# A streaming column sum on one core: tapering the last loads, folding half of the accumulator early, and splitting the final copy

## Chip, cores and metric

The kernel runs on one core of a Trainium2 chip. The metric is the device time in microseconds (us) of that core, as the median of several executions. "Span" is the length of the one profiled execution by the profiler's clock; it is some 1.8 us shorter than the time of the same execution.

## The reference

```python
def setup_inputs():
    batch, seq, dim = 32, 1024, 2048
    return {"grad_output": np.random.randn(batch, seq, dim).astype(np.float32)}

def reference(grad_output):
    return np.sum(grad_output, axis=(0, 1)).astype(np.float32)
```

So 32,768 rows of 2048 fp32 values are summed to one row: 268 MB come in and 8 KB go out.

## The kernel before

The rows come in as 128 buffers of 256 rows, two rows per partition (2 MB each, 16 KB contiguous per partition), through a ring of five buffers. Of each buffer VectorE (DVE) adds the first row of every partition to an accumulator `acc` of 128 x 2048. TensorE (PE) sums the second row over the partitions by a matmul with a column of ones, into the first partition of `ps`, in four chunks of 512 columns. At the end PE folds `acc` into `ps` in the same way, one DVE instruction copies `ps` to `res`, and one transfer sends it out.

```python
    for i in range(NBUF):                                   # NBUF = 128
        buf = sbuf.tile([P, Q, D], f32, tag="inbuf")        # Q = 2, bufs=5
        rows = flat[i * P * Q : (i + 1) * P * Q]
        nc.sync.dma_start(out=buf[:], in_=rows.rearrange("(p q) d -> p q d", p=P))
        for t in range(Q):
            if t % 2 == 0:
                nc.vector.tensor_add(acc[:], acc[:], buf[:, t])
            else:
                pe_quantum(buf[:, t])          # 4 matmuls of 512 columns (line 46)

    for k in range(NK):                        # fold: 4 matmuls on acc (line 66)
        nc.tensor.matmul(ps[0:1, k * 512 : (k + 1) * 512], ones[:],
                         acc[:, k * 512 : (k + 1) * 512], start=not started[k], stop=True)

    res = const.tile([1, D], f32)
    nc.vector.tensor_copy(res[0:1], ps[0:1, :D])            # line 75
    nc.sync.dma_start(out=out[None, :], in_=res[0:1])       # line 76
```

Of the kernel before, what the change touches and what calls it, by code (L numbers as in the profile page):

```python
# [1 line left out]

# [4 lines left out]


@with_exitstack  # L10
def kernel(
    ctx: ExitStack,
    tc: tile.TileContext,
    grad_output: bass.AP,
    out: bass.AP,
):
    nc = tc.nc
    P = nc.NUM_PARTITIONS
    f32 = mybir.dt.float32

    flat = grad_output.flatten_outer_dims()
    N, D = flat.shape
    assert D == out.shape[-1]

    Q = 2
    NBUF = N // (P * Q)
    assert N % (P * Q) == 0
    NK = (D + 511) // 512
    assert D % 512 == 0

    sbuf = ctx.enter_context(tc.tile_pool(name="sbuf", bufs=5))
    const = ctx.enter_context(tc.tile_pool(name="const", bufs=1))
    psum = ctx.enter_context(tc.tile_pool(name="psum", bufs=1, space=bass.MemoryType.PSUM))

    acc = const.tile([P, D], f32)
    ones = const.tile([P, 1], f32)
    nc.vector.memset(acc[:], 0.0)  # L37
    nc.any.memset(ones[:], 1.0)  # L38

    ps = psum.tile([P, NK * 512], f32)  # L40

    started = [False] * NK

    def pe_quantum(q_ap):
        for k in range(NK):
            nc.tensor.matmul(  # L46
                ps[0:1, k * 512 : (k + 1) * 512],
                ones[:],
                q_ap[:, k * 512 : (k + 1) * 512],
                start=not started[k],  # L50
                stop=False,
            )
            started[k] = True

    for i in range(NBUF):
        buf = sbuf.tile([P, Q, D], f32, tag="inbuf")
        rows = flat[i * P * Q : (i + 1) * P * Q]
        nc.sync.dma_start(out=buf[:], in_=rows.rearrange("(p q) d -> p q d", p=P))  # L58
        for t in range(Q):
            if t % 2 == 0:  # L60
                nc.vector.tensor_add(acc[:], acc[:], buf[:, t])  # L61
            else:
                pe_quantum(buf[:, t])

    for k in range(NK):
        nc.tensor.matmul(  # L66
            ps[0:1, k * 512 : (k + 1) * 512],
            ones[:],
            acc[:, k * 512 : (k + 1) * 512],
            start=not started[k],  # L70
            stop=True,
        )

    res = const.tile([1, D], f32)
    nc.vector.tensor_copy(res[0:1], ps[0:1, :D])  # L75
    nc.sync.dma_start(out=out[None, :], in_=res[0:1])


# [1 line left out]
_INS = ['grad_output']  # L80
_OUTS = [((2048,), 'float32')]


# [23 lines left out]
```

## Time and profile before

| what | value | where |
|---|---|---|
| time, median of the first 4 runs | 645.27 us (645.11 to 645.57) | timed runs |
| span of the profiled execution | 643.8 us | page |
| the profiled execution's own time | 645.57 us, 0.36 over the median of all 13 runs (645.21) | timed runs |
| bytes in, mean rate over the span | 268 MB, 417 GB/s | page |
| landing of the last load | 632.1 us | chain of waits |
| from there to the end of the span | 11.7 us | chain, timeline |

These are lines of the page of the kernel before: the span, the busy time of each engine, the busy share of the DMA engines and their rate in 40 equal slices of the span, and the shares of the chain that ended last.

```profile
span 643.8 us, 2622 instructions
...
PE 464.6 (72%) x1032; PEld 76.0 (12%) x1032; DVE 297.4 (46%) x130; POOL 0.3 (0%) x5
...
DMA  8999999999999999999999999999999999999991
GB/s 360 432 430 423 432 429 427 428 429 428 427 428 431 425 428 432 427 428 430 428 428 428 432 426 427 434 425 428 432 425 427 429 430 425 430 431 426 427 433 58
...
DMA 84%; PE 15%; DVE 0%; issue 0%; SPq 0%
```

The DMA engines are busy 90% or more (the digit 9) from the second slice to the last but one, at about 428 GB/s. PE looks busy at 72%, but it waits for loads (174.6 us in all, by the page). The 15% of PE in the chain is misleading: in mid-stream the chain passes through PE because PE frees the buffers (123 of the waits of the queue that issues loads end with PE, 153.3 us in all), and four more loads are then outstanding (a load lands 20.8 us after its issue, one every 4.89 us). The interesting slice is the last, where DMA shows 1 and 58 GB/s: the stream is over and something else still runs.

This is the timeline of the kernel before at its end. The columns are start (us), duration (us), engine, line, operation, output<-inputs, shapes and count; in brackets, how long the engine was idle before it and what ended that. "SPq" is the queue that issues transfers.

```profile
622.39 3.59 PE L46 MATMUL ps<-buf,ones 128*1 128x512 f32 x8 [1.30 <-DMA buf<-in_grad_output_dram]
...
627.29 3.59 PE L46 MATMUL ps<-buf,ones 128*1 128x512 f32 x8 [1.31 <-DMA buf<-in_grad_output_dram]
...
632.16 3.59 PE L46 MATMUL ps<-buf,ones 128*1 128x512 f32 x8 [1.27 <-DMA buf<-in_grad_output_dram]
632.21 2.29 DVE L61 TENSOR_TENSOR acc<-acc,buf 128x2048 f32<-128x2048 f32 x1 [2.57 <-DMA buf<-in_grad_output_dram]
...
635.59 3.60 PE L66 MATMUL ps<-acc,ones 128*1 128x512 f32 x8
...
639.22 2.28 DVE L75 COPY res<-ps 1x2048 f32<-1x2048 f32 x1 [4.72 <-PE ps L66]
641.53 0.31 SPq L76 DMA_DIRECT2D out_dram<-res  x1
```

A buffer lands every 4.89 us. PE needs 3.6 us of that and DVE 2.29, so each waits for the next landing. Each fp32 matmul of 512 columns appears as two records ("x8" for four chunks), called passes below; they start 0.43 us apart.

The chain of waits of the same execution shows the tail without overlaps (start, duration, what):

```profile
611.32 20.79 DMA buf<-in_grad_output_dram
632.11 0.04 issue
632.16 3.59 PE ps L46 x8
635.75 3.45 PE ps L66 x8
639.20 0.02 issue
639.22 2.28 DVE res L75
```

After the last landing come 16 PE passes (7.04 us), the copy (2.28 us), and the output with the end of the program (2.26 us). None of this overlaps a load, so all of it is time that a change can win.

### The profile page before, as it was taken

The page shows a single profiled execution, that of the slowest core. Times are in us where ns is not written, and L with a number is a line of the kernel's source. Part 1 is how long each engine was busy: PE and PEld are TensorE (multiplying, and loading weights), DVE is VectorE, ACT ScalarE, POOL GpSimd, SP SyncE. Part 2 cuts the span into 40 slices and gives each one's busy share as a digit, 9 for nine tenths or more (in the row PEclk, how much of TensorE's full clock was granted, in tenths as well). Part 3 has the DMA queues.
Part 4 walks back from the last instruction along what each step waited for, and adds up shares of the span by engine and source line. Part 5 has one row for each costly group of instructions (what it writes and reads, how often), then busy time and mean ns, then how long its engine had stood idle before and what let it go on. Part 6 is the DMA issues. An engine that isn't in the chain of part 4 may idle for free.

```text
span 643.8 us, 2622 instructions
## 1 busy us (share of the span) xinstructions
PE 464.6 (72%) x1032; PEld 76.0 (12%) x1032; DVE 297.4 (46%) x130; POOL 0.3 (0%) x5
## 2 busy tenths in 40 slices
PE   4776776777777677777767777776777677677766
PEld 0111111111111111111111111111111111111111
DVE  3444544544454454445445444544544454445444
POOL 0000000000000000000000000000000000000000
PEclk9999999999999999999999999999999999999999
DMA  8999999999999999999999999999999999999991
GB/s 360 432 430 423 432 429 427 428 429 428 427 428 431 425 428 432 427 428 430 428 428 428 432 426 427 434 425 428 432 425 427 429 430 425 430 431 426 427 433 58
DMA packets 18446, 268.62 MB, mean 417 GB/s; under 512 B 2049, under 2 KB 2049, under 8 KB 2049
## 3 DMA queue, kind: packets, MB, share of 16 engines
q1 hardware_dynamic: 18434, 268.45, 98.1%
q8 instruction: 8, 0.13, 0.1%
q14 instruction: 4, 0.03, 0.0%
HBM read 268.44 MB, written 0.01 MB: 417 GB/s over the span
## 4 chain that ended last, share of the span: by engine, by line
DMA 84%; PE 15%; DVE 0%; issue 0%; SPq 0%
DMA buf<-in_grad_output_dram 84%; PE ps L46 15%; PE ps L66 1%; DVE res L75 0%; SPq L58 0%
## 5 line engine op out<-in xcount | busy, mean ns | idle before, releaser
L46 PE MATMUL ps<-buf,ones 128*1 128x512 f32 x1024 | 461.2, 593 | 174.6 <-DMA buf<-in_grad_output_dram 174.6
L61 DVE TENSOR_TENSOR acc<-acc,buf 128x2048 f32<-128x2048 f32 x128 | 293.4, 2292 | 338.1 <-DMA buf<-in_grad_output_dram 338.1
L46 PEld LDWEIGHTS ps<-buf,ones 128*1 128x1 f32 x1024 | 75.4, 83 | 559.5 <-DMA buf<-in_grad_output_dram 284.5
L75 DVE COPY res<-ps 1x2048 f32<-1x2048 f32 x1 | 2.3, 2279 | 4.7 <-PE ps L66 4.7
L66 PE MATMUL ps<-acc,ones 128*1 128x512 f32 x8 | 3.6, 592 | 0.0
L37 DVE MEMSET acc<- 128x2048 f32 x1 | 1.8, 1765 | 1.2 <-PEq L91 1.2
L66 PEld LDWEIGHTS ps<-acc,ones 128*1 128x1 f32 x8 | 0.7, 84 | 2.8 <-issue 2.8
L91 POOL MEMSET const-bfloat16-1.0<- 128x1 bf16 x1 | 0.1, 101 | 0.0
L91 POOL MEMSET const-uint8-127<- 128x1 uint8 x1 | 0.1, 101 | 0.0
L38 POOL MEMSET ones<- 128x1 f32 x1 | 0.1, 98 | 0.3 <-POOLq L91 0.3
L91 POOL MEMSET const-float32-0.0<- 128x1 f32 x1 | 0.1, 98 | 0.2 <-issue 0.2
L91 POOL MEMSET const-float32-1.0<- 128x1 f32 x1 | 0.1, 98 | 0.0
## 6 DMA issues: line engine op xcount, KB each, us to landing
buf<-in_grad_output_dram SPq DMA_DIRECT2D x128, 2048.0 KB, 20.8
out_dram<-res SPq DMA_DIRECT2D x1, 8.0 KB
```

The source lines that it names most:

```text
L37: nc.vector.memset(acc[:], 0.0)
L38: nc.any.memset(ones[:], 1.0)
L46: nc.tensor.matmul(ps[0:1, k * 512 : (k + 1) * 512], ones[:], q_ap[:, k * 512 : (k + 1) * 512], start=not started[k], stop=False,)
L61: nc.vector.tensor_add(acc[:], acc[:], buf[:, t])
L66: nc.tensor.matmul(ps[0:1, k * 512 : (k + 1) * 512], ones[:], acc[:, k * 512 : (k + 1) * 512], start=not started[k], stop=True,)
L75: nc.vector.tensor_copy(res[0:1], ps[0:1, :D])
L91: nc = _bacc.Bacc("TRN2", target_bir_lowering=False, num_devices=1)
```

## The change

The intent is to shorten that tail without touching the stream. The change does three things:

1. **Taper the loads.** The last 512 rows come as three loads of 128 rows (1 MB), then the last 128 rows in three column pieces of 0.5, 0.25 and 0.25 MB.
2. **Fold early.** After the fourth-last 2 MB buffer PE folds columns 1024 to 2047 of `acc`. From then on, so in the last three 2 MB buffers and the taper, PE takes those columns of every row directly, and DVE takes columns 0 to 1023 alone. So only two chunks are left to fold at the end.
3. **Split the copy.** ScalarE (ACT) copies columns 1024 to 2047 and then 512 to 1023; DVE copies the last 512.

It also replaces the clearing of `acc` by a copy of the first buffer.

```diff
-    NBUF = N // (P * Q)
+    NBULK = (N - 4 * P) // (P * Q)        # 126
+    SWITCH = NBULK - 4
 ... (helpers: dma() loads rows or a column piece; pe() sums chunks of a row directly; fold() sums chunks of acc)
+    for i in range(NBULK):
+        buf = dma(P * Q, Q)
+        if i == 0:
+            nc.vector.tensor_copy(acc[:], buf[:, 0])
+            pe(buf, 1, LO + HI)                       # LO = chunks 0, 1; HI = chunks 2, 3
+        elif i <= SWITCH:
+            nc.vector.tensor_add(acc[:], acc[:], buf[:, 0])
+            pe(buf, 1, LO + HI)
+            if i == SWITCH:
+                fold(HI, stop=False)
+        else:
+            nc.vector.tensor_add(acc[:, 0:H], acc[:, 0:H], buf[:, 0, 0:H])
+            nc.vector.tensor_add(acc[:, 0:H], acc[:, 0:H], buf[:, 1, 0:H])
+            pe(buf, 0, HI)
+            pe(buf, 1, HI)
+    for _ in range(3):
+        bufc = dma(P, 1)
+        nc.vector.tensor_add(acc[:, 0:H], acc[:, 0:H], bufc[:, 0, 0:H])
+        pe(bufc, 0, HI)
+    bhi = dma(P, 1, dlo=H, dhi=D)
+    b1 = dma(P, 1, dlo=512, dhi=H)
+    b0 = dma(P, 1, dlo=0, dhi=512)
+    pe(bhi, 0, HI, stop=True, doff=H)
+    nc.vector.tensor_add(acc[:, 512:H], acc[:, 512:H], b1[:, 0])
+    fold([1], stop=True)
+    nc.vector.tensor_add(acc[:, 0:512], acc[:, 0:512], b0[:, 0])
+    fold([0], stop=True)
-    nc.vector.tensor_copy(res[0:1], ps[0:1, :D])
+    nc.scalar.copy(res[0:1, H:D], ps[0:1, H:D])
+    nc.scalar.copy(res[0:1, 512:H], ps[0:1, 512:H])
+    nc.vector.tensor_copy(res[0:1, 0:512], ps[0:1, 0:512])
```

## The prediction

> **What bounds the kernel.** The load stream. In the page's slices the DMA engines are 90% or more busy almost throughout, at about 428 GB/s, and the chain of waits is 84% DMA. [...] A 2 MB buffer lands each 4.89 us (timeline: 622.39, 627.29, 632.16). Per buffer PE is busy 3.59 us (eight passes, 0.43 us apart), DVE 2.29 us: both have slack. Bytes do not change, so only the ends of the span can. The start cannot: the first load is issued at 0.73 us, and the removed memset ran before the first landing (8.5 us).
>
> **The tail before** (timeline): last landing 632.16; PE on that buffer to 635.6; fold of acc to 639.19; DVE copy of 2048 elements on one partition, 2.28 us, to 641.5; output DMA and end 2.25 us, 643.8. That is 11.6 us, all critical.
>
> **What the change does.** Last loads shrink (three of 1 MB, 0.5 MB, two of 0.25 MB), columns 1024 to 2047 are folded earlier, and the final copy is split: 1024+512 on ACT, 512 on DVE. Estimates from the durations above, landings spaced by bytes:
> - Smaller loads have smaller packets. [...] no view of this trace shows 2 KB packets. I estimate 0.3 us: last landing 632.4, the last 1 MB load about 629.9. The last load's buffer is free (about 628) 4 us before it must land.
> - PE, not the last load, then bounds the tail. From 629.9: 4 passes for the 1 MB load, 4 for the 0.5 MB load (landed 631.2), 2+2 for the two folds: 12 × 0.43 + 0.16 = 5.3 us, to 635.3. The chain through the last load would be ready earlier: add of 512 elements about 0.65 us, to 633.1, while PE is still on earlier work. Some 1.3 us of the ideal gain is lost to PE's backlog.
> - DVE copy of 512: about 0.65 us (a quarter of 2.28 plus start-up), to 636.0. ACT's copies, about 1.0 and 0.6 us, lie beside PE's last passes.
> - Output DMA and end unchanged, 2.25 us: 638.2.
>
> The early fold (4 passes, 1.7 us) fits in the slack of 1.3 us per buffer; with four loads outstanding it does not starve the stream.
>
> So the span falls by 5.5 us, from 643.8 to 638.2, and the time from 645.27 to about **639.7 us** (0.9% less). Range for 8 in 10: 638.7 to 641.3. Chances: faster by over 2% 0.01, within 2% 0.98, slower 0.01.
>
> **What would show each step.** (1) Landings still 4.89 us apart, the last at 632.2 to 633. (2) PE without idle time from the last 1 MB load's landing to the last fold; that fold waits on PE order, not on DVE. (3) DVE copy near 0.65 us, starting about 635.3. (4) Span ends 2.2 to 2.3 us after the output is issued. (5) The chain's last pieces: a load, PE's passes, a short DVE copy, output.
>
> **What would make it wrong.** Small loads landing over 1.2 us late: then the tail is load, add, fold, copy. PE passes slower than 0.43 us. A late-issued small load that leaves the queue empty. ACT's copies outlasting PE's folds. A table load for ACT that disturbs the start. A gain over 2% (13 us) is not possible: the whole tail is 11.6 us.

## The result, and the profile after

The changed kernel takes 639.79 us (median of 8 runs, 639.57 to 639.99), against 645.21 us (13 runs) for the kernel before. The ratio is 0.9915, with a 95% interval of 0.9906 to 0.9925. Ratios here are not quite the ratio of the medians. The change wins 5.4 us, or 0.85%.

The page of the changed kernel, the same lines as before:

```profile
span 638.0 us, 2640 instructions
...
PE 467.0 (73%) x1032; PEld 76.6 (12%) x1032; DVE 293.9 (46%) x135; ACT 2.8 (0%) x3; POOL 0.3 (0%) x5
...
DMA  8999999999999999999999999999999999999995
GB/s 363 428 430 430 427 428 429 427 426 427 427 428 428 425 430 430 427 429 428 429 428 428 427 426 427 428 428 427 430 428 427 428 428 426 429 430 427 428 422 213
```

The stream's rate is the same, and the busy times hardly differ. What changed is the last slice: the DMA engines are busy for half of it, not for a tenth.

The end of its chain of waits, and then its timeline from the last 1 MB load on (weight loads left out):

```profile
616.14 13.33 DMA buf<-in_grad_output_dram
629.47 0.04 issue
629.52 3.59 PE ps L64 x8
633.11 1.73 PE ps L75 x4
634.84 0.02 issue
634.87 0.68 DVE res L116
```

```profile
629.52 3.59 PE L64 MATMUL ps<-buf,ones 128*1 128x512 f32 x8 [0.44 <-DMA buf<-in_grad_output_dram]
629.57 1.22 DVE L102 TENSOR_TENSOR acc<-acc,buf 128x1024 f32<-128x1024 f32 x1 [1.26 <-DMA buf<-in_grad_output_dram]
...
631.44 0.69 DVE L109 TENSOR_TENSOR acc<-acc,buf 128x512 f32<-128x512 f32 x1 [0.65 <-DMA buf<-in_grad_output_dram]
...
632.05 0.68 DVE L111 TENSOR_TENSOR acc<-acc,buf 128x512 f32<-128x512 f32 x1
...
632.95 1.88 PE L75 MATMUL ps<-acc,ones 128*1 128x512 f32 x4
...
633.15 1.00 ACT L114 COPY res<-ps 1x1024 f32<-1x1024 f32 x1 [631.13 <-PE ps L64]
...
634.06 0.57 ACT L115 COPY res<-ps 1x512 f32<-1x512 f32 x1
634.87 0.68 DVE L116 COPY res<-ps 1x512 f32<-1x512 f32 x1 [2.14 <-PE ps L75]
635.62 0.32 SPq L117 DMA_DIRECT2D out_dram<-res  x1
```

The load in the chain is no longer the last one; it is the last 1 MB load, landed at 629.47. From 629.52 PE runs twelve passes without a gap, to 634.84. The very last load landed at 631.99 (the trace's semaphore events, which `prof` does not list); DVE begins to add it at 632.05, and that add is done at 632.73. PE comes to that chunk's fold only 1.1 us later. So the last load is not what the end waits for: PE's queue of passes is.

The two chains account for the difference (each number is taken or subtracted from lines above):

| part of the tail | before | after | difference |
|---|---|---|---|
| start of PE's last unbroken run | 632.16 | 629.52 | -2.64 |
| PE passes in it | 16: 7.04 us | 12: 5.32 us | -1.72 |
| start of the DVE copy to issue of the output | 2.31 us | 0.75 us | -1.56 |
| issue of the output to end of span | 2.26 us | 2.41 us | +0.16 |
| sum | | | -5.76 (spans, unrounded: -5.75) |

The profiled execution of before was 0.36 us above its median, and this lies in the first row: its loads landed late by about that much (copy_only below has the same loads, in an execution at its median, and its last one landed 0.47 us earlier). Without it the sum is -5.4 us, as the medians say. The start does not enter: PE begins on the first buffer at 8.55 us before and at 8.53 after. ACT's one table load, which the trace puts at the line of its first copy, took 1.28 us from 0.73 on and was over before DVE began on the first buffer at 8.42.

### The profile page after: what moved, and what is told of

Same layout as the page of the kernel before. It is cut to its first block, busy times and chain, and to the rows that moved or that the text cites. A ratio compares the mean times of both kernels' runs of the same rounds, so it can differ in the third digit from the quotient of the medians.

```text
span 638.0 us, 2640 instructions
## 1 busy us (share of the span) xinstructions
PE 467.0 (73%) x1032; PEld 76.6 (12%) x1032; DVE 293.9 (46%) x135; ACT 2.8 (0%) x3; POOL 0.3 (0%) x5
## 4 chain that ended last, share of the span: by engine, by line
DMA 82%; PE 18%; issue 0%; DVE 0%
DMA buf<-in_grad_output_dram 82%; PE ps L64 17%; PE ps L75 1%; DVE res L116 0%
## 5 line engine op out<-in xcount | busy, mean ns | idle before, releaser
L90 DVE TENSOR_TENSOR acc<-acc,buf 128x2048 f32<-128x2048 f32 x122 | 279.6, 2292 | 320.4 <-DMA buf<-in_grad_output_dram 320.4
L95 DVE TENSOR_TENSOR acc<-acc,buf 128x1024 f32<-128x1024 f32 x3 | 3.7, 1225 | 7.4 <-DMA buf<-in_grad_output_dram 7.4
L102 DVE TENSOR_TENSOR acc<-acc,buf 128x1024 f32<-128x1024 f32 x3 | 3.7, 1225 | 2.5 <-DMA buf<-in_grad_output_dram 2.5
L114 ACT COPY res<-ps 1x1024 f32<-1x1024 f32 x1 | 1.0, 1001 | 631.1 <-PE ps L64 631.1
L96 DVE TENSOR_TENSOR acc<-acc,buf 128x1024 f32<-128x1024 f32 x3 | 3.7, 1225 | 0.1
L109 DVE TENSOR_TENSOR acc<-acc,buf 128x512 f32<-128x512 f32 x1 | 0.7, 691 | 0.6 <-DMA buf<-in_grad_output_dram 0.6
L111 DVE TENSOR_TENSOR acc<-acc,buf 128x512 f32<-128x512 f32 x1 | 0.7, 682 | 0.0
```

Of the source, the lines that this page charges most:

```text
L90: nc.vector.tensor_add(acc[:], acc[:], buf[:, 0])
L95: nc.vector.tensor_add(acc[:, 0:H], acc[:, 0:H], buf[:, 0, 0:H])
L96: nc.vector.tensor_add(acc[:, 0:H], acc[:, 0:H], buf[:, 1, 0:H])
L102: nc.vector.tensor_add(acc[:, 0:H], acc[:, 0:H], bufc[:, 0, 0:H])
L109: nc.vector.tensor_add(acc[:, 512:H], acc[:, 512:H], b1[:, 0])
L111: nc.vector.tensor_add(acc[:, 0:512], acc[:, 0:512], b0[:, 0])
```

## Experiments

Theory A says that the tail is the sum in this table and that, in the changed kernel, PE's backlog of passes bounds it. Rival B says that the chain through the last load (land, add, fold, copy) bounds it; then PE work could be added for free and DVE work could not. A second rival asked whether one part alone (the loads, say) brings all the gain. All twelve runs gave right results.

The runs came each with runs of the kernel before on the same chip. The intervals of the ratios are wide, 0.6 to 1.1 us to each side, and overlap from row to row. Differences of 0.6 to 1 us between versions of the changed kernel rest on single runs that do not overlap (639.55 to 639.99 for the changed kernel, 640.38 to 640.79 for pe_plus, 638.82 to 639.29 for presum) and on the traces:

| run | median, us | minus before | ratio to before (95%) |
|---|---|---|---|
| copy_only | 643.63 | -1.52 | 0.9977 (0.9964 to 0.9989) |
| fold_only | 643.35 | -1.80 | 0.9972 (0.9959 to 0.9984) |
| loads_only | 643.05 | -2.10 | 0.9967 (0.9954 to 0.9979) |
| pe_plus | 640.55 | -4.60 | 0.9929 (0.9916 to 0.9943) |
| dve_plus1 | 639.72 | -5.42 | 0.9915 (0.9900 to 0.9930) |
| dve_plus3 | 639.77 | -5.37 | 0.9916 (0.9901 to 0.9931) |
| presum | 639.12 | -6.02 | 0.9906 (0.9892 to 0.9921) |
| presum_out | 639.06 | -6.08 | 0.9905 (0.9888 to 0.9921) |
| dve_chain3 | 640.82 | -4.41 | 0.9932 (0.9919 to 0.9944) |
| after_again (the changed kernel) | 639.78 | -5.45 | 0.9914 (0.9900 to 0.9928) |
| presum_again | 639.17 | -6.06 | 0.9905 (0.9892 to 0.9919) |
| presum_out_again | 638.96 | -6.27 | 0.9903 (0.9889 to 0.9916) |

### One part at a time

**copy_only**: the kernel before with the copy split.

```diff
-    nc.vector.tensor_copy(res[0:1], ps[0:1, :D])
+    nc.scalar.copy(res[0:1, 0:1024], ps[0:1, 0:1024])
+    nc.scalar.copy(res[0:1, 1024:1536], ps[0:1, 1024:1536])
+    nc.vector.tensor_copy(res[0:1, 1536:2048], ps[0:1, 1536:2048])
```

> The kernel before with the final copy alone split (ACT copies 1024 and 512 columns, DVE the last 512). If the three parts of the tail simply add, the last fold still ends 7.0 us after the last landing (639.2 on the profile), then a copy of 0.68 us takes the place of 2.28 us: 1.6 us less, about 643.6 us, span 642.2. If ACT's copies (1.00 and 0.57 us as the changed kernel's profile has them) do not fit beside PE's last passes, the output waits for ACT and the gain is smaller. If all the gain comes from the loads, no change: 645.2 us.

Measured: 1.52 us less. In its timeline the last DVE copy takes 0.68 us, and ACT's second copy ends at 638.5, before that copy starts (638.75).

**fold_only**: the early fold with all loads at 2 MB and one copy.

```diff
 (against the changed kernel)
-    NBULK = (N - 4 * P) // (P * Q)
+    NBULK = N // (P * Q)
 ... (the taper is left out; the last buffer's pe() closes chunks 2 and 3)
+    fold([1, 0], stop=True)
+    nc.vector.tensor_copy(res[0:1], ps[0:1, :D])
```

> The early fold alone: in the last four buffers DVE takes columns 0 to 1023 and PE columns 1024 to 2047, the accumulator's upper half is folded before them, all loads stay 2 MB and one DVE copy of 2048 columns ends it. If PE's passes in order bound the tail, the last landing stays at 632.1 and 12 passes (5.3 us) follow it in place of 16 (7.0 us): 1.7 us less, about 643.5 us. If the early fold held the stream back, the last landing would be later than 632.2 and the gain would be lost.

Measured: 1.80 us less. (The edit changes the last three buffers, not four as the expectation says.) The profile has the last landing at 631.5, and then twelve passes in 5.32 us. The stream was not held back.

**loads_only**: the tapered loads, with the fold of all four chunks at the end and one copy.

```diff
 (against the changed kernel)
-            if i == SWITCH:
-                fold(HI, stop=False)
 ... (SWITCH = NBULK: no drain stage)
-    pe(bhi, 0, HI, stop=True, doff=H)
+    pe(bhi, 0, HI, doff=H)
+    fold(HI, stop=True)
 ...
+    nc.vector.tensor_copy(res[0:1], ps[0:1, :D])      (in place of the three copies)
```

> The smaller last loads alone: three of 1 MB, one of 0.5 MB, two of 0.25 MB, with DVE on columns 0 to 1023 and PE on the rest of them, but no early fold and one DVE copy of 2048 columns. If PE's passes in order bound the tail, PE starts its unbroken run of passes at the landing of the last 1 MB load (629.5) and needs 16 of them: 636.6, then copy 2.28 us: 2.6 us less than before, about 642.6 us. If the chain through the last load counted, the fold of the last columns would wait for DVE's add of the last load (632.7) and end 1.0 us after it, and the gain would be over 5 us (640 us or less).

Measured: 2.10 us less, 0.5 us short of the figure, yet the steps are those expected, as the end of its chain of waits shows:

```profile
629.20 3.59 PE ps L62 x8
632.80 3.45 PE ps L73 x8
636.24 0.02 issue
636.27 2.28 DVE res L111
```

PE starts at the last 1 MB landing and runs 16 passes in 7.04 us. The expectation of 2.6 us was set against the profiled execution of before, which was 0.36 us slower than its median. Its output also took 0.16 us longer from issue to end (2.41 against 2.26). 2.64 - 0.36 - 0.16 is 2.1.

The three parts alone win 1.52 + 1.80 + 2.10 = 5.42 us; the whole change wins 5.42. They add, as parts do that shorten different links of one serial chain; that they agree to the last digit is luck, since each median is good to some 0.1 us. No single part holds the gain.

### Which engine bounds the new tail

**pe_plus**: one matmul more (two passes) before the last folds, into a spare bank.

```diff
     pe(bhi, 0, HI, stop=True, doff=H)
+    nc.tensor.matmul(spare[0:1, :], ones[:], bhi[:, 0, 0:512], start=True, stop=True)
```

> The changed kernel with one more matmul of 512 columns (two passes, 0.86 us) into a spare bank just before the last folds. If PE's backlog bounds the tail, all of it shows: 0.86 us more than the changed kernel, about 640.65 us. If the chain through the last load (land, add, fold, copy) bounds it, as the rival has it, the extra passes fit in front of DVE's last add and the time stays at 639.8 us.

Measured: 4.60 us less than before, where the changed kernel wins 5.42 to 5.45. So the two passes cost about 0.8 us of their 0.86: PE has next to no slack in the tail. B fails here. Lines of its chain of waits, with the added passes in line:

```profile
629.21 3.59 PE ps L65 x8
632.80 0.86 PE spare L110 x2
633.66 1.73 PE ps L76 x4
```

**dve_plus1** and **dve_plus3**: one or three adds more on DVE, into a spare tile.

```diff
     fold([1], stop=True)
+    for _ in range(1):      (3 in dve_plus3)
+        nc.vector.tensor_add(spare[:], b1[:, 0], b1[:, 0])
     nc.vector.tensor_add(acc[:, 0:512], acc[:, 0:512], b0[:, 0])
```

> The changed kernel with one more DVE add of 512 columns (0.6 to 0.7 us, into a spare tile) before DVE's add of the last load. In the changed kernel's profile that last add ends at 632.7, and PE comes to the last fold at 633.8: 1.1 us of slack. If PE's backlog bounds the tail, nothing changes: 639.8 us. If the chain through the last load bounds it, 0.6 to 0.7 us more: 640.4 us.

> The same with three more adds, 1.9 us. If PE's backlog bounds the tail with 1.1 us of slack for DVE, only the part beyond the slack shows: 0.8 us more, about 640.6 us, and the last fold's first pass then waits for DVE. If the chain through the last load bounds it, all 1.9 us: 641.7 us.

Measured: dve_plus1 costs nothing (-5.42), as A has it, though DVE's add of the last load started 0.6 us later than in the changed kernel (632.65 against 632.05):

```profile
632.05 0.68 DVE L113 TENSOR_TENSOR spare<-buf 128x512 f32<-128x512 f32 x1
632.65 0.68 DVE L114 TENSOR_TENSOR acc<-acc,buf 128x512 f32<-128x512 f32 x1
```

dve_plus3 costs nothing either (-5.37), and A had expected 0.8 us. Its timeline of DVE shows why:

```profile
631.55 0.69 DVE L110 TENSOR_TENSOR acc<-acc,buf 128x512 f32<-128x512 f32 x1 [0.65 <-DMA buf<-in_grad_output_dram]
632.16 0.69 DVE L113 TENSOR_TENSOR spare<-buf 128x512 f32<-128x512 f32 x1
632.76 0.69 DVE L114 TENSOR_TENSOR acc<-acc,buf 128x512 f32<-128x512 f32 x1
633.37 1.41 DVE L113 TENSOR_TENSOR spare<-buf 128x512 f32<-128x512 f32 x2
```

The add of the last load (line 114) stands second: in the program as built, two of the three spare adds come behind it, and nothing in the source forbade that order. The run was thus no test of three adds. An experiment that adds work must tie it into the chain by data.

**dve_chain3**: the same, mended. The three extra instructions now write what the last add reads.

```diff
     fold([1], stop=True)
+    nc.vector.tensor_sub(zero[:], b1[:, 0], b1[:, 0])
+    nc.vector.tensor_add(acc[:, 0:512], acc[:, 0:512], zero[:])
+    nc.vector.tensor_add(acc[:, 0:512], acc[:, 0:512], zero[:])
     nc.vector.tensor_add(acc[:, 0:512], acc[:, 0:512], b0[:, 0])
```

> The run with three extra DVE adds, mended: there the compiler put two of them behind the add of the last load, so it delayed nothing. Here the three (b1 minus b1, and its zeros added to the accumulator twice) write and read what the last add needs, and so must stand before it. The last add then ends at about 634.7 in place of 632.7, and PE is ready for the last fold at 633.8. If PE's backlog bounds the tail with 1.1 us of slack for DVE, only the part beyond the slack shows: the fold's two passes (1.02 us) follow at 635.8 in place of 634.85, 0.8 to 1.0 us more than the changed kernel of the same call. If the chain through the last load bounds it, all 2.0 us.

> The changed kernel itself, as control of this call: 639.8 us, ratio to before 0.9915.

Measured: 1.04 us more than the changed kernel beside it (640.82 against 639.78). DVE's last add started 1.94 us later than in that control (634.01 against 632.07), and the span of that execution was 0.92 us longer than the control's (638.96 against 638.04), so about 1.0 us of the delay was slack, near the 1.1 us read off the changed kernel's timeline. Lines of its timeline:

```profile
634.01 0.69 DVE L115 TENSOR_TENSOR acc<-acc,buf 128x512 f32<-128x512 f32 x1
...
634.75 1.02 PE L76 MATMUL ps<-acc,ones 128*1 128x512 f32 x2 [1.01 <-DVE acc L115]
635.81 0.68 DVE L120 COPY res<-ps 1x512 f32<-1x512 f32 x1 [1.11 <-PE ps L76]
```

Now PE does wait, 1.01 us, for DVE. This is what B's world looks like, and it had to be made. It also shows the two kinds of bracket: in the changed kernel the passes of the folds carry no wait at all, here there is one of a microsecond.

### A version with less PE work in the tail

If PE's passes bound the tail, taking two away should help. In **presum** the 0.5 MB piece comes as two of 0.25 MB. For chunk 2 DVE, which has slack, adds the last 1 MB load's row to the last block's row first, and PE sums the two rows in one matmul.

```diff
-    for _ in range(3):
+    for n in range(3):
         bufc = dma(P, 1)
         nc.vector.tensor_add(acc[:, 0:H], acc[:, 0:H], bufc[:, 0, 0:H])
-        pe(bufc, 0, HI)
+        pe(bufc, 0, HI if n < 2 else [3])
-    bhi = dma(P, 1, dlo=H, dhi=D)
 ... (b3, b2, b1, b0: 0.25 MB each, in tiles of their own)
-    pe(bhi, 0, HI, stop=True, doff=H)
+    pe(b3, 0, [3], stop=True, doff=3 * 512)
+    nc.vector.tensor_add(b2[:, 0], b2[:, 0], bufc[:, 0, H : H + 512])
+    pe(b2, 0, [2], stop=True, doff=2 * 512)
```

> A correct version with less PE work in the tail: the 0.5 MB load is cut in two, and for columns 1024 to 1535 DVE adds the row of the last 1 MB load to the row of the last block first, so that PE does these columns in two passes, not four. If PE's backlog bounds the tail, 10 passes follow the last 1 MB landing in place of 12; by the landings (629.5, 630.1) and DVE's add (ready 631.4) the last fold then ends at about 634.15 in place of 634.85: 0.7 us less, about 639.1 us. If the chain through the last load bounds it, DVE's added work makes it 0.6 us slower or leaves it: 639.8 to 640.4 us.

> The version with less PE work again, beside the changed kernel on one chip: 0.65 us less than it (639.1 us), if the first comparison was right.

Measured: 639.12 us (-6.02 against before), and beside the changed kernel 639.17 against 639.78: 0.61 us less. Of this some 0.53 us is PE's shorter run of passes (4.79 us, from 629.41 to 634.20, against 5.32 us) and 0.07 us the end of the program (2.34 us against 2.41; see the last part of the next section). DVE got one add more in the tail and the kernel got faster, which B does not allow. In the timeline of PE the new limit is visible:

```profile
629.41 1.02 PE L70 MATMUL ps<-buf,ones 128*1 128x512 f32 x2 [0.44 <-DMA buf<-in_grad_output_dram]
630.27 1.02 PE L70 MATMUL ps<-last,ones 128*1 128x512 f32 x2
631.45 1.02 PE L70 MATMUL ps<-last,ones 128*1 128x512 f32 x2 [0.16 <-DVE last L113]
632.31 1.88 PE L81 MATMUL ps<-acc,ones 128*1 128x512 f32 x4
```

The third row starts on a wait of 0.16 us for DVE's presum: the two engines are now nearly level, so moving more to DVE would win little (an estimate from that wait; no run tried it).

**presum_out** also sends columns 512 to 2047 early from ACT's queue, so that the last transfer is 2 KB.

```diff
     nc.scalar.copy(res[0:1, 512:H], ps[0:1, 512:H])
+    nc.scalar.dma_start(out=out[None, 512:D], in_=res[0:1, 512:D])
     nc.vector.tensor_copy(res[0:1, 0:512], ps[0:1, 0:512])
-    nc.sync.dma_start(out=out[None, :], in_=res[0:1])
+    nc.sync.dma_start(out=out[None, 0:512], in_=res[0:1, 0:512])
```

> The same, and the output is sent as two: columns 512 to 2047 from ACT's queue as soon as they are copied, the last 512 by the last transfer. The single output packet of 8 KB took about 0.31 us; a 2 KB one should take less than 0.1. If only the size of the last transfer counts, 0.2 us less than the version without it, about 638.9 us; if the end waits on something that does not depend on the size, no change.

> The version with the output in two, again beside the one without. In the first pair the time from the issue of the last transfer to the end of the span fell from 2.33 to 2.11 us, but the whole by only 0.06 us, within its spread. If the shorter output counts, 0.2 us less than the version without it; if the 0.06 us are all, the rest is taken back elsewhere or lies in the spread of the stream.

Measured: 0.06 us less than presum in the second call and 0.21 less in the third. In the profiles the time from the last issue to the end of the span fell from 2.3 us (637.3 - 634.97; 637.0 - 634.68) to 2.1 us (637.2 - 635.13; 637.3 - 635.14) both times, as estimated. The single runs of these kernels spread over 0.23 to 0.45 us, so the whole time does not settle 0.1 to 0.2 us. There it points the right way and is not shown.

The traces give a reading that leaves out where the stream happens to end: the time from PE's start on the last 1 MB load to the end of the span.

| kernel | us in its profiles | against the changed kernel |
|---|---|---|
| the changed kernel (after, after_again) | 8.51, 8.50 | |
| dve_plus1, dve_plus3 | 8.51, 8.51 | 0.0 |
| pe_plus | 9.37 | +0.86 |
| dve_chain3 | 9.67 | +1.17 |
| presum, presum_again | 7.89, 7.90 | -0.61 |
| presum_out, presum_out_again | 7.62, 7.60 | -0.90 |

So pe_plus pays for its two passes in full, dve_chain3 for the 2.19 us by which its last add comes later on this clock less 1.0 us of slack, and the early output does shorten the tail, by 0.28 us against presum.

The lowest medians are those of presum_out: ratio to before 0.9903 to 0.9905, some 0.8 us under the changed kernel (638.96 against 639.78).

## Why the prediction was right

The prediction gave 639.7 us, and the runs give 639.79. Point by point:

- **What bounds the kernel.** Right. The rate stayed at about 428 GB/s and only the last slice changed. Whether a higher rate is to be had was not shown: no run tried it.
- **PE, not the last load, bounds the new tail.** Right, and tested: two passes more cost 0.8 us (pe_plus), one DVE add more costs nothing (dve_plus1), three in series cost 1.04 us, about 1.0 us less than they delay the last add (dve_chain3), and two passes fewer win 0.6 us (presum).
- **The sizes.** Last 1 MB landing: predicted 629.9, seen 629.47. Twelve passes: 5.3, seen 5.32. DVE copy: 0.65, seen 0.68. ACT copies: 1.0 and 0.6, seen 1.00 and 0.57. Issue to end: 2.25, seen 2.41. Span: 638.2, seen 638.0. The 0.3 us for the smaller loads and the times of the ACT copies were the author's estimates, with nothing in the trace of before to work them out from.
- **The early fold.** Right that it does not starve the stream, but its 1.7 us did not fit in one buffer's slack of 1.3 us; it took part of the next one's. Its four passes made PE start the next buffer at 612.51, 0.25 us after that landed; one buffer later PE waited for the load again (617.15, idle 1.04 us), and landings stayed 4.89 us apart.
- **The last load is issued in time.** Right: predicted about 628, and the last issue ended at 627.7, over 4 us ahead of its landing.
- **Where it was off.** The landing's 0.4 us comes mainly from reading the start off one profiled execution that was 0.36 us slower than its kernel's median. This cost the time nothing, since the prediction subtracted a difference from the median. Two of the ranges given in advance were missed: the last landing (632.2 to 633, seen 631.99, for the same reason) and the end after the output's issue (2.2 to 2.3 us, seen 2.41). The output's extra 0.16 us was not foreseen. That the total still came within 0.1 us is partly luck: the median of before fell from 645.27 to 645.21 us with more runs, and the last 1 MB load came up to 0.1 us earlier than predicted once the 0.36 us is allowed for.

The page of the changed kernel has the durations closer: DVE's copy of 512 elements from `ps` took 679 ns, ACT's copies of 1024 and 512 took 1001 and 569 ns, DVE's add of 512 columns 691 and 682 ns. DVE's copy of 2048 elements in the kernel before took 2279 ns; a straight line through its two sizes gives, as an estimate, 0.15 us of start-up and 1.04 ns per element.

**The end of the program.** From the output's issue to the end of the span (by the trace's unrounded spans) every kernel with the change's tapered loads took 2.40 to 2.41 us, the three without them (before, copy_only, fold_only) 2.26 to 2.32, and presum, which cuts the last piece further, 2.34. No run was made for this, but the semaphore events in the kept traces place it. The 8 KB output lands 1.38 to 1.40 us after its issue in all of them (the 2 KB one of presum_out after 1.16). After that SyncE, the engine that issues the transfers, still steps through the rest of a list of semaphore waits, some 0.065 us apart: one in before and fold_only, two in copy_only, three in presum, four in the kernels with the tapered loads. From landing to end of span they took 0.87, 0.93, 0.95 and 1.02 us. So the extra 0.16 us comes after the output has landed; what gives the output's semaphore its place in that list stays open.

## What to carry to other kernels

In this kernel the stream ran at its rate and its start was left alone, so the gain lay in the part of the chain after the stream ends. List its links from the timeline and add them: links in series can be shortened one by one, as the three parts here were (1.52 + 1.80 + 2.10 = 5.42 us). When the last loads are cut small, ask how fast each engine consumes a piece: where, as here, one piece lands 0.64 us after another (the last two, at 631.34 and 631.99 by the trace's semaphore events) and an engine needs 0.86 us for it (PE's two passes), the queue of that engine, not the last byte, ends the kernel, and work should move to the engine with slack (in presum, 0.61 us). Finally, an experiment that adds work to see who waits has to be tied into the dependences, or it may end up where it costs nothing, as in dve_plus3.

## Further figures from these traces

- Small loads behind others: issued by SyncE in such a queue, the 0.5 and the first 0.25 MB load had both landed 1.87 us after the last 1 MB load (DVE's starts, 629.57 and 631.44): 786 KB in 1.87 us, about 420 GB/s, against 429 for the 2 MB loads (2 MB in 4.89 us).
- Packets: the smaller loads have smaller ones. The changed kernel's trace has 256 of 2 KB and 128 of 4 KB, and that of before has none of either. In its packet records the medians are 84 ns for 2 KB, 159 for 4 KB, 313 for 8 KB and 613 for 16 KB: by a straight line through them, an estimate of some 9 ns per packet beyond the bytes.
- An fp32 matmul of 512 columns is two records 0.43 us apart, 0.86 us in all.
- The end of the program: issued by SyncE, an 8 KB output landed 1.38 to 1.40 us after its issue and the span ended 2.26 to 2.41 us after it; with a last transfer of 2 KB it was 1.16 and 2.11 us.
